# Weight splitting, staging copies and B/K scaling move between VectorE, ScalarE and GpSimd in a one-core hybrid decoder step, under another planner clock

## The chip, the cores and the metric

The program runs on 1 core of one Trainium2 chip. The metric is device microseconds of one execution; the times before are the median of three runs. The names of the engines in the profile are PE (TensorE matmul), PEld (TensorE weight load), DVE (VectorE), ACT (ScalarE), POOL (GpSimd) and SP (SyncE, which here only issues transfers).

## The reference

One step of a decoder layer for a 1024-token prompt and 8 sequences of 4 sampled tokens: one input projection feeds an RWKV-7 branch (a recurrence with a 64x64 state for each of 16 heads) and an RG-LRU branch; both are gated, merged, projected, normed and sent through a SwiGLU FFN.

```python
z = jnp.einsum('btd,de->bte', x, w_in)
...
# RWKV-7, for each token and head
sa = jnp.einsum('bhij,bhj->bhi', S, -kk_t)
S = (S * w_t[:, :, None, :]
     + sa[..., None] * (kk_t * a_t)[:, :, None, :]
     + v_t[..., None] * k_t[:, :, None, :])
y_t = jnp.einsum('bhij,bhj->bhi', S, r_t)
...
merged = (gate_a * yA + gate_b * yB).astype(x.dtype)
mix = jnp.einsum('bte,ed->btd', merged, w_o)
h1 = _layer_norm(ALPHA * x + mix, ln1_g, ln1_b)
ffn = (jax.nn.silu(h1 @ w_ffn_gate) * (h1 @ w_ffn_up)) @ w_ffn_down
y = _layer_norm(ALPHA * h1 + ffn, ln2_g, ln2_b)
```

Everything is fp32. The large products are made from two parts of each operand: a high part that TensorE's fast fp32 format holds, and the low part that is left; three products (high-high, high-low, low-high) are added up.

## The kernel before, in words

**Weights.** `Weights` streams weight tiles of 128x8x128 through two buffers `wraw`, loaded by transfers that the GpSimd queue issues. `split` cuts each tile in two halves of 128x512. ScalarE copies a half to the high part `wh` (`A`), then the low part `wl` is `wraw - wh`: by VectorE for half 0 (`TT`), by GpSimd for half 1 (`PTT`; `ON_POOL = 1,`). Weight tiles 0 to 115 belong to the input projection, 116 to 131 to the output projection `wo`, and the others to the FFN.

**The first part** (up to about 1475 us of the trace) makes the input projection in two passes, the first over samples and tokens 0 to 511 (matmuls of 300, 292 and 256 columns), the second over tokens 512 to 1023 (512 columns). `STREAM` lists the order of its groups as (kind, unit): kind 0 is `r` and `k`, 1 is `v`, 2 is the LRU's input, 3 the three gates; a unit is two 128-row channel blocks, that is four heads, in one pass, so that there are eight units. While TensorE works down this list, the recurrence of each unit runs beside it in steps:

- `wkv_tile` makes the decayed keys and queries on ScalarE and VectorE (tiles `tmp`, `rge`, `kta`).
- `stage(u, g)` copies them for half g of a unit (four chunks of 64 tokens) to `bk` and `arm`: for each of 2 blocks and 2 heads, ScalarE makes two copies of 64x256 and VectorE two (`TS` by 1.0). There are 16 such halves.
- `inverse(u, g)` makes products of these on TensorE, sends `nz` through DRAM (`scrN` to `bn`), solves 16x16 triangles on VectorE with 30 small operations (`btmp`, `bt`), and brings the result back through DRAM (`scrT` to `tdv`, `scrZ` to `zt`). These transfers go through SP's queue. In the lists below `scrN_172`, `scrT_176`, `scrZ_174` belong to half 0 and `scrN_173`, `scrT_177`, `scrZ_175` to half 1.
- `chain(u)` is the recurrence, 8 steps a unit. In a step TensorE makes `cx` from `arm` and the state `su`, ScalarE and VectorE copy it to `xs`, TensorE makes `cu`, both copy it to `su`, TensorE makes `cs_` from `bkt` and `su`, and VectorE adds four 64x64 pieces of the state for the next step. `ahead(c)` prepares step c: VectorE scales `bk` by a column of `pc` into `bkh` (twice 128x128), and TensorE transposes it.
- `finish`, `gate_out` and `lru` norm, gate and make the other branch. `bonus_weights` copies two tiles of 128x512 or 128x548 per unit to `rkk` on GpSimd.

`arm`, `bk` and `rb` have one buffer: a half is staged only once the chain of the unit before has passed the same half.

**The FFN** (1475 to 2190 us) is one dense run of matmuls with weight splitting beside it, and a last norm ends the program.

**Order.** No engine's order is written out. A planner (`Ticker`) emits the instructions of all tasks one by one; on each engine they run in the order in which they were emitted. It keeps a model of time (`Clock`): each instruction gets a cost, and the task whose next instruction could start earliest is emitted next. Between matmuls of the dense stream `tick` puts in what the model holds to be ready. Two parts of that model matter here: `clocked` doubles the cost of matmuls in a 3.413 us window after one with little work (a TensorE clock at half speed), and `shared` lengthens a VectorE operation by 0.7 of its overlap with one on GpSimd. Every instruction that the planner emits for a task has line L333 in the profile, those of the main stream L263; the buffers' names (`wl`, `bkh`) tell them apart.

Of the kernel before, what the change touches and what calls it, by code (L numbers as in the profile page):

```python
# [9 lines left out]
F32 = mybir.dt.float32  # L10
# [35 lines left out]
ON_POOL = 1,  # L46
G_RK, G_V, G_XB, G_GATE = range(4)
STREAM = [(0, 0), (1, 0), (1, 1), (0, 1), (2, 0), (3, 0), (0, 2), (2, 1), (3, 1), (0, 3), (2, 2), (1, 2), (3, 2), (2, 3), (1, 3), (3, 3), (0, 4), (1, 4), (1, 5), (0, 5), (2, 4), (3, 4), (2, 5), (0, 6), (3, 5), (2, 6), (2, 7), (0, 7), (1, 6), (3, 6), (1, 7), (3, 7)]
# [28 lines left out]
class Clock:  # L77
# [6 lines left out]
    def __init__(self):  # L84
        self.t = dict.fromkeys(("PE", "ACT", "DVE", "POOL", "SP", "DMA"), 0.0)
        self.uses = {}
        self.masks = {}
        self.table = 0
        self.tile = None
        self.port = {"DVE": [], "POOL": []}  # L90
        self.window, self.work, self.half = 0, 0.0, True
# [30 lines left out]
    def cost(self, e, f, out, ins, args, kw):  # L122
        n = max(self.size(x) for x in [out] + ins[:1])
        sbuf = all(x.space == SB for x in [out] + ins)
        if e == "PE":
            if f == "transpose":
                return 0.109
            k, m, n = args[1].shape[0], args[1].shape[1], self.size(args[2])
            if args[1].dtype == F32R:
                return max(0.11, n / 2250)  # L130
            if k <= 32:
                return 0.045
            return max(m, n) / 600 if m == 128 else max(0.09, n / 1000)
# [15 lines left out]
    WINDOW = 3.413  # L149

    def clocked(self, at, n, share):

        while at >= self.WINDOW * (self.window + 1):
            self.half = self.work < self.WINDOW * (0.7 if self.half else 0.45)
            self.window += 1
            self.work = 0.0
        n *= 1 + self.half
        self.work += min(n, self.WINDOW * (self.window + 1) - at) * share
        return n

    def shared(self, e, f, out, ins, at, end):

        if f == "memset" or e == "DVE" and (any(x.space != SB for x in ins) or f == "tensor_tensor_scan"):
            return 0.0
        port = self.port[e]
        port.append((at, end))
        del port[:-12]
        over = sum(max(0.0, min(end, b) - max(at, a)) for a, b in self.port["POOL" if e == "DVE" else "DVE"])
        if e == "DVE":
            return 0.7 * over  # L170
        self.t["DVE"] += 0.7 * over
        return 0.0
# [21 lines left out]
    def op(self, e, f, args, kw, at, last):  # L194
# [8 lines left out]
        else:  # L203
            if e == "PE":
# [4 lines left out]
                self.tile = tile  # L209
            end = at + self.FIXED[e] + self.cost(e, f, out, ins, args, kw)  # L210
            if e == "PE":
                share = 1.0 if min(tile) > 3 else 0.1 if max(tile) < 2 else 0.6
                end = at + self.clocked(at, end - at, share)
            if e in self.port:
                end += self.shared(e, f, out, ins, at, end)
# [147 lines left out]
def tile_hybrid_step(ctx: ExitStack, tc: tile.TileContext, I, O):  # L363
# [65 lines left out]
    class Weights:  # L429
# [21 lines left out]
        def split(self):  # L451
            for j, (_, nk) in enumerate(self.srcs):
# [3 lines left out]
                for part in range(self.PARTS):  # L456
                    k = slice(part * nk // self.PARTS, (part + 1) * nk // self.PARTS)
                    A(h[:, k], raw[:, k])
                    (PTT if part in ON_POOL else TT)(l[:, k], raw[:, k], h[:, k].bitcast(F32), OP.subtract)
# [35 lines left out]
    with ExitStack() as zctx:  # L495
# [240 lines left out]
        def bonus_weights(u, ts):  # L736
            while u > 0 and (u - 1, "fin") not in F:
                yield
            for i, t in enumerate(ts):
                pool.tensor_scalar(rkk[:, i, span(units[u][0])], t[:, span(units[u][0])], 1.0, None, op0=OP.mult)  # L740
                temps.put(t)
# [100 lines left out]
        def stage(u, g, n2, parts):  # L842
# [5 lines left out]
            for i, (t1, t4, t5) in enumerate(parts):  # L848
                cs, ts = slice(4 * g, 4 * g + 4), slice(PO + 256 * g, PO + 256 * g + 256)
                for h in range(2):  # L850
                    s = slice(64 * h, 64 * h + 64)
                    A(bk[s, i, cs, 1 - h, :], t1[s, ts].rearrange(ch, t=64))
                    TS(bk[s, i, cs, h, :], t4[s, ts].rearrange(ch, t=64), 1.0)
                    A(arm[s, i, cs, h, 0, :], kzs[u][s, i, ts].rearrange(ch, t=64))
                    TS(arm[s, i, cs, h, 1, :], rzs[u][s, i, ts].rearrange(ch, t=64), 1.0)
# [148 lines left out]
        def chain(u):  # L1004
# [7 lines left out]
            def ahead(c):  # L1012

                if c >= 0:
                    for i in range(2):
                        TS(bkh[:, i], bk[:, i, c], pc[:, i, c:c + 1], None, op0=OP.mult)
# [961 lines left out]
```

## Time and profile before

| | before |
|---|---|
| median of 3 runs | 2242.56 us (2242.42 to 2244.06) |
| the profiled execution | 2241.18 us, of which the profile's span 2239.2 us |
| instructions | 44150 |
| PE / PEld busy | 2094.6 us (94%) / 1805.1 us (81%) |
| DVE / ACT / POOL busy | 1303.2 us (58%) / 992.5 us (44%) / 592.5 us (26%) |
| mean granted TensorE clock | 0.950 |
| HBM | 132.45 MB read, 17.57 MB written, 67 GB/s |

The profile is of one execution. Shares of a whole span hide that the first part and the FFN differ; the views by stretch of time (windows) and the chain of waits tell them apart. In a row of a group, the number behind x is the count, then come the busy time in us and the mean of one in ns, then the idle time before it with what ended it. A fp32 matmul of the recurrence counts as two matmuls in the profile.

### The profile page before, as it was taken

The page shows a single profiled execution, that of the slowest core. Times are in us where ns is not written, and L with a number is a line of the kernel's source. Part 1 is how long each engine was busy: PE and PEld are TensorE (multiplying, and loading weights), DVE is VectorE, ACT ScalarE, POOL GpSimd, SP SyncE. Part 2 cuts the span into 40 slices and gives each one's busy share as a digit, 9 for nine tenths or more (in the row PEclk, how much of TensorE's full clock was granted, in tenths as well). Part 3 has the DMA queues.
Part 4 walks back from the last instruction along what each step waited for, and adds up shares of the span by engine and source line. Part 5 has one row for each costly group of instructions (what it writes and reads, how often), then busy time and mean ns, then how long its engine had stood idle before and what let it go on. Part 6 is the DMA issues. An engine that isn't in the chain of part 4 may idle for free.

```text
span 2239.2 us, 44150 instructions
## 1 busy us (share of the span) xinstructions
PE 2094.6 (94%) x17664; PEld 1805.1 (81%) x17664; DVE 1303.2 (58%) x3123; ACT 992.5 (44%) x2220; POOL 592.5 (26%) x961
## 2 busy tenths in 40 slices
PE   7899789989999999899989889999999999999997
PEld 6898688987977776666667678889999999999986
DVE  4785876986967476887967755632322322223227
ACT  4556555756555457556585433752112121121221
POOL 3331232331513331231422313221211211212124
PEclk9997899999979999989999989999999999999999
DMA  4131121231321232131322433211111111111111
GB/s 132 62 105 42 36 74 49 71 92 53 117 72 42 88 95 58 60 84 38 92 60 62 130 96 120 104 67 37 58 48 37 49 49 33 62 38 48 57 38 78
DMA packets 125564, 152.83 MB, mean 68 GB/s; under 512 B 82912, under 2 KB 87424, under 8 KB 125360
## 3 DMA queue, kind: packets, MB, share of 16 engines
q0 software_dynamic: 32576, 112.75, 14.9%
q1 hardware_dynamic: 92784, 37.28, 6.7%
q8 instruction: 138, 2.26, 0.4%
q14 instruction: 66, 0.54, 0.1%
HBM read 132.45 MB, written 17.57 MB: 67 GB/s over the span
## 4 chain that ended last, share of the span: by engine, by line
PE 65%; DVE 23%; ACT 7%; issue 3%; DMA 2%; POOL 0%; SPq 0%; POOLq 0%; DVEq 0%; ACTq 0%
PE bank L263 52%; PE bank L333 12%; DVE tmp L333 5%; DVE wl L333 2%; DVE arm L333 2%; DVE btmp L333 2%; DVE bt L333 2%; ACT tmp L333 1%; DVE yb L333 1%; DVE rge L333 1%; DVE su L333 1%; DVE bk L333 1%; ACT wh L333 1%; DVE rb L333 1%; ACT L333 1%
## 5 line engine op out<-in xcount | busy, mean ns | idle before, releaser
L263 PE MATMUL bank<-xx,wh 128*128 128x512 f32 (+4 forms) x3168 | 811.8, 343 | 32.7 <-ACT xx L263 8.6
L263 PEld LDWEIGHTS bank<-xx,wh 128*128 128x128 f32 x3168 | 553.4, 196 | 95.8 <-issue 19.0
L333 POOL TENSOR_TENSOR wl<-wraw,wh 128x512 fp32r<-128x512 f32 (+2 forms) x212 | 276.6, 1305 | 1178.0 <-ACT wh L333 1063.5
L263 PE MATMUL bank<-xx,wl 128*128 128x512 f32 (+4 forms) x1584 | 541.2, 342 | 0.3 <-DVE wl L333 0.3
L333 ACT ACTIVATE wh<-wraw 128x512 fp32r<-128x512 f32 (+2 forms) x424 | 249.9, 599 | 300.3 <-PE bank L263 265.7
L263 PE MATMUL bank<-hh,wh 128*128 128x272 f32 (+1 forms) x1056 | 341.8, 324 | 1.3 <-ACT hh L333 1.3
L263 PE MATMUL bank<-hl,wh 128*128 128x272 f32 (+1 forms) x1056 | 342.8, 325 | 0.2 <-DVE hl L333 0.2
L263 PE MATMUL bank<-hh,wl 128*128 128x272 f32 (+1 forms) x1056 | 341.9, 324 | 0.0
L263 PEld LDWEIGHTS bank<-xx,wl 128*128 128x128 f32 x1584 | 310.0, 196 | 31.2 <-issue 4.1
L333 DVE TENSOR_TENSOR wl<-wraw,wh 128x512 fp32r<-128x512 f32 (+1 forms) x212 | 187.5, 884 | 248.4 <-ACT wh L333 247.5
L263 PEld LDWEIGHTS bank<-hh,wh 128*128 128x128 f32 x1056 | 199.0, 188 | 18.1 <-ACT hh L333 1.8
L263 PEld LDWEIGHTS bank<-hl,wh 128*128 128x128 f32 x1056 | 198.9, 188 | 16.4 <-DVE hl L333 0.5
L263 PEld LDWEIGHTS bank<-hh,wl 128*128 128x128 f32 x1056 | 198.8, 188 | 15.5
L263 PE MATMUL bank<-u,wh 128*128 128x272 f32 (+1 forms) x864 | 197.5, 322 | 0.0
L263 PEld LDWEIGHTS bank<-u,wh 128*128 128x128 f32 x864 | 143.8, 188 | 12.9
L333 DVE TENSOR_TENSOR acc<-acc,bank 128x272 f32<-128x272 f32 (+3 forms) x120 | 62.2, 519 | 137.0 <-PE bank L263 135.2
L263 PE MATMUL bank<-u,wl 128*128 128x272 f32 (+1 forms) x432 | 139.4, 323 | 0.0
L333 DVE TENSOR_TENSOR sg<-sg,bank 128x272 f32<-128x272 f32 (+1 forms) x66 | 34.4, 521 | 159.7 <-PE bank L263 159.7
L333 ACT ACTIVATE sg<-bank 128x272 f32<-128x272 f32 (+1 forms) x66 | 30.7, 465 | 195.8 <-PE bank L263 195.8
L333 ACT ACTIVATE su<-bank 64x256 f32<-64x256 f32 (+1 forms) x192 | 60.0, 338 | 82.8 <-PE bank L333 78.8
L333 DVE SCALAR_TENSOR_TENSOR su<-su,pc,bank 64x64 f32<-64x64 f32 x224 | 62.7, 280 | 44.3 <-PE bank L333 39.3
L263 PEld LDWEIGHTS bank<-u,wl 128*128 128x128 f32 x432 | 81.2, 188 | 6.1
(249 smaller groups left out, 3185.4 us busy)
## 6 DMA issues: line engine op xcount, KB each, us to landing
wraw<-in_win POOLq DMA_DIRECT2D x116, 512.0 KB, 3.6
wraw<-in_wgu POOLq DMA_DIRECT2D x48, 512.0 KB, 3.6
wraw<-in_wo POOLq DMA_DIRECT2D x16, 512.0 KB, 3.6
wraw<-in_wdn POOLq DMA_DIRECT2D x24, 256.0 KB, 2.9
wraw<-in_wdn POOLq DMA_DIRECT2D x16, 320.0 KB, 3.2
mgd<-yb POOLq DMA_DIRECT2D x32, 128.0 KB, 2.5
out_y<-tmp SPq DMA_DIRECT2D x8, 512.0 KB
scrN<-nz SPq DMA_DIRECT2D x64, 32.0 KB
```

Source lines behind the costliest of these rows:

```text
L263: fn(*args, **kw)
L333: fn(*args, **kw)
```

## The change

Four pieces of work move and the planner's model changes:

- `split`: for weight tiles with j < `N_IN` = 132 (input projection and `wo`) both low halves are subtracted by VectorE; for the FFN's tiles half 1 stays on GpSimd.
- `stage`: the two VectorE copies become ScalarE copies, so that ScalarE makes all four.
- `ahead`: `bkh` is scaled by ScalarE (an activation with a scale column) instead of VectorE.
- `bonus_weights`: the copies to `rkk` go from GpSimd to ScalarE.
- `Clock`: the model of the half-speed TensorE clock goes (`clocked`); instead of a stretch by overlap, an operation of VectorE or GpSimd that uses the shared port waits until the one that holds it ends (`locked`). A cost of small matmuls changes from 0.09 to 0.08, and `STREAM` is another order of the same 32 groups.

```diff
-ON_POOL = 1,
+ON_POOL, N_IN = (1,), 132
 G_RK, G_V, G_XB, G_GATE = range(4)
-STREAM = [(0, 0), (1, 0), (1, 1), (0, 1), (2, 0), (3, 0), (0, 2), (2, 1), (3, 1), (0, 3), (2, 2), (1, 2), (3, 2), (2, 3), (1, 3), (3, 3), (0, 4), (1, 4), (1, 5), (0, 5), (2, 4), (3, 4), (2, 5), (0, 6), (3, 5), (2, 6), (2, 7), (0, 7), (1, 6), (3, 6), (1, 7), (3, 7)]
+STREAM = [(0, 0), (1, 0), (0, 1), (2, 0), (1, 1), (3, 0), (2, 1), (0, 2), (3, 1), (2, 2), (1, 2), (0, 3), (3, 2), (2, 3), (1, 3), (3, 3), (0, 4), (1, 4), (2, 4), (0, 5), (1, 5), (2, 5), (3, 4), (0, 6), (3, 5), (2, 6), (0, 7), (1, 6), (1, 7), (3, 6), (2, 7), (3, 7)]
...
-            return max(m, n) / 600 if m == 128 else max(0.09, n / 1000)
+            return max(m, n) / 600 if m == 128 else max(0.08, n / 1000)
...
-    WINDOW = 3.413
-
-    def clocked(self, at, n, share):
...
-    def shared(self, e, f, out, ins, at, end):
...
+    def locked(self, e, f, out, ins, at):
+
+        if f in ("memset", "tensor_reduce", "tensor_tensor_scan") or e == "DVE" and any(x.space != SB for x in [out] + ins):
+            return at, False
+        for a, b in self.port["POOL" if e == "DVE" else "DVE"]:
+            if a <= at < b:
+                at = b
+        return at, True
...
+            lock = False
+            if e in self.port:
+                at, lock = self.locked(e, f, out, ins, at)
             end = at + self.FIXED[e] + self.cost(e, f, out, ins, args, kw)
-            if e == "PE":
-                share = 1.0 if min(tile) > 3 else 0.1 if max(tile) < 2 else 0.6
-                end = at + self.clocked(at, end - at, share)
-            if e in self.port:
-                end += self.shared(e, f, out, ins, at, end)
+            if lock:
+                self.port[e] = self.port[e][-8:] + [(at, end)]
...
-                    (PTT if part in ON_POOL else TT)(l[:, k], raw[:, k], h[:, k].bitcast(F32), OP.subtract)
+                    (PTT if part in ON_POOL and j >= N_IN else TT)(l[:, k], raw[:, k], h[:, k].bitcast(F32), OP.subtract)
...
-                pool.tensor_scalar(rkk[:, i, span(units[u][0])], t[:, span(units[u][0])], 1.0, None, op0=OP.mult)
+                A(rkk[:, i, span(units[u][0])], t[:, span(units[u][0])])
...
-                    TS(bk[s, i, cs, h, :], t4[s, ts].rearrange(ch, t=64), 1.0)
+                    A(bk[s, i, cs, h, :], t4[s, ts].rearrange(ch, t=64))
...
-                    TS(arm[s, i, cs, h, 1, :], rzs[u][s, i, ts].rearrange(ch, t=64), 1.0)
+                    A(arm[s, i, cs, h, 1, :], rzs[u][s, i, ts].rearrange(ch, t=64))
...
-                        TS(bkh[:, i], bk[:, i, c], pc[:, i, c:c + 1], None, op0=OP.mult)
+                        A(bkh[:, i], bk[:, i, c], AF.Copy, pc[:, i, c:c + 1])
```

Because the planner sets the order, every engine's order changes. Three places follow. (In the changed file the planner's helper is line L316 instead of L333 and the main stream's L246 instead of L263.)

The first is SP's queue in unit 0. Before, half 1 (`scrN_173`) is sent out and its `bn` read back ahead of half 0 (`scrN_172`):

```order
L333 DMA scrN_173<-nz 32x8x32
L333 DMA tmp_96<-scrS 4x128
L333 DMA scrN_173<-nz 32x8x32 x3
L333 DMA scrX<-tmp_96 4x128
L333 DMA bn<-scrN_173 32x16x16 x2
L333 DMA zc_170<-scrX 32x2x4 x2
L333 DMA scrN_172<-nz 32x8x32
```

and in the changed kernel:

```order
L316 DMA scrN_172<-nz 32x8x32
L316 DMA tmp_94<-in_lora 128x256
L316 DMA scrN_172<-nz 32x8x32 x3
L316 DMA bn<-scrN_172 32x16x16 x2
L316 DMA scrS<-sc_169 32x2x4 x2
L316 DMA tmp_96<-scrS 4x128
L316 DMA scrN_173<-nz 32x8x32 x2
```

Half 0, on which the chain of unit 0 waits, now goes first.

The second is TensorE's queue at the first step of unit 3's chain, the last unit of the first pass. `su_149,arm` is `cx`, `xs,nz` is `cu`, `su_149,bkt_155` is `cs_`; rows with `xx` are the dense stream. Before:

```order
L333 MATMUL bank_71<-su_149,arm 64x64 x4
L333 MATMUL bank_68<-tdv,nz 32x16
L333 MATMUL bank_67<-tmp 128x256
L263 MATMUL bank_65<-xx,wh_78 128x292 x2
L333 MATMUL bank_70<-cst,vz_126 128x128 x2
L333 MATMUL bank_70<-cst,bkh 128x128 x2
L333 MATMUL bank_71<-xs,nz 64x64 x4
L333 MATMUL bank_68<-zt,p_139 32x16 x32
L333 MATMUL bank_68<-p_139,zt 32x16 x6
L333 MATMUL bank_71<-su_149,bkt_155 64x64 x4
```

and in the changed kernel, from a few rows behind `cx` on:

```order
L316 MATMUL bank_69<-tmp 128x256
L316 MATMUL bank_70<-cst,vz_126 128x128 x2
L316 MATMUL bank_70<-cst,bkh 128x128 x2
L316 MATMUL bank_71<-xs,nz 64x64 x4
L316 MATMUL bank_67<-tmp 32x64 x2
L246 MATMUL bank_66<-xx,wl_79 128x512
L246 MATMUL bank_66<-xx,wh_77 128x512
L316 MATMUL bank_68<-tmp 128x292
L246 MATMUL bank_66<-xx,wh_77 128x512
L246 MATMUL bank_66<-xx,wl_79 128x512
L246 MATMUL bank_66<-xx,wh_77 128x512 x2
L316 MATMUL bank_71<-su_149,bkt_155 64x64 x4
```

Before, the first pass's last tiles (292 columns) stand here; now the second pass's first tiles (512 columns) stand ahead of this chain and in it. Counted over all rows, the stream's matmuls between the last `cs_` of one chain and the first of the next, and within the chains, are:

| stretch of TensorE's order | before | after |
|---|---|---|
| ahead of chain 0 | 954 | 730 |
| chain 0 to chain 1 | 184 | 512 |
| chain 1 to chain 2 | 656 | 524 |
| chain 2 to chain 3 | 432 | 504 + 62 of 512 columns |
| chain 3 to chain 4 (512 columns, but 8 before) | 484 | 320 |
| in chains 0, 1, 2 | 150, 134, 150 | 188, 164, 162 |
| in chain 3 | 116 | 80 of 512 columns |
| in chains 4, 5, 6 (512 columns) | 100, 92, 108 | 130, 104, 120 |

The third is the same chain step on the engines that carry `bkh`. Before, VectorE's queue:

```order
L333 TENSOR_SCALAR bkh<-bk,pc_135 128x128 x2
L333 COPY xs<-bank_71 64x2x64
L333 TENSOR_SCALAR bkh<-bk,pc_135 128x128 x2
L333 COPY su_149<-bank_71 64x2x64
L333 SCALAR_TENSOR_TENSOR su_150<-su_149,pc_135,bank_71 64x64 x4
L333 TENSOR_TENSOR tdv<-tdv,bank_68 32x8x16 x2
```

In the changed kernel, ScalarE's queue:

```order
L316 ACTIVATE xs<-bank_71 64x2x64
L316 ACTIVATE bkh<-bk,pc_135 128x128
L316 ACTIVATE wh_78<-wraw_76 128x512
L316 ACTIVATE rge_199<-bank_65,omu 128x512
L316 ACTIVATE bkh<-bk,pc_135 128x128
L316 ACTIVATE tmp<-bank_67 32x64 x2
L316 ACTIVATE wh_78<-wraw_76 128x512
L316 ACTIVATE tmp_94<-bank_68,dv 128x292
L316 ACTIVATE tmp_94<-bank_69,dv 128x256
L316 ACTIVATE su_149<-bank_71 64x2x64
```

`bkh` now shares ScalarE's queue with the splitting of weights and with copies out of the stream's banks, and the second `bkh` stands behind one of each.

More of the change, by code (lines that the diff above doesn't have):

```diff
@@ L90, in __init__ @@
         self.port = {"DVE": [], "POOL": []}
-        self.window, self.work, self.half = 0, 0.0, True
     def mask(self, ap):
@@ L147, in cost @@
         return max(0.1, n / {"tensor_tensor": 450, "tensor_scalar": 330, "tensor_copy": 300}.get(f, 1150))
-    WINDOW = 3.413
-    def clocked(self, at, n, share):
[L153 to L159, printed above, removed]
-    def shared(self, e, f, out, ins, at, end):
[L163 to L172, printed above, removed]
+    def locked(self, e, f, out, ins, at):
[5 more added lines that the diff above has]
+        return at, True
     def accesses(self, args, kw):
```

## The prediction

> **What bounds the kernel now.** I read the page's engine shares and its chain of waits first, then the same by stretch of time, then the groups of VectorE, ScalarE and GpSimd in the first part, then single rows.
>
> ```profile
> PE 2094.6 (94%) x17664; PEld 1805.1 (81%) x17664; DVE 1303.2 (58%) x3123; ACT 992.5 (44%) x2220; POOL 592.5 (26%) x961
> PE 65%; DVE 23%; ACT 7%; issue 3%; DMA 2%; POOL 0%; SPq 0%; POOLq 0%; DVEq 0%; ACTq 0%
> 0.00:1475.00 1475.00, 1346.75 (x13047) 1129.15 (x13048) 1068.12 (x2723) 837.80 (x1907) 434.06 (x781) 0.93 0.26 78
> 1475.00:2190.00 715.00, 715.00 (x4360) 644.47 (x4359) 195.59 (x311) 146.99 (x297) 135.58 (x164) 1.00 0.15 47
> 1474.52 715.64 PE bank L263 x4359
> ```
>
> The second row is the chain of waits; the windows' columns are the stretch, its length, the busy time of PE, PEld, DVE, ACT and POOL, the granted clock, the DMA share and GB/s. From 1475 to 2190 us TensorE is busy all the time at full clock and is one piece of the chain. Nothing that the change touches bounds it there, and the FFN keeps its splitting. So VectorE's 23% of the chain (515 us) and ScalarE's 7% (157 us) lie nearly all in the first 1475 us: 35% and 11% of them. In that part VectorE is busy 72%, ScalarE 57%, and the clock is 0.93. The first part is bound by two things in turn: TensorE's own work, and the recurrence's way through VectorE, ScalarE and the transfers, which leaves TensorE with too little to do in places.
>
> **Work that moves, engine by engine.** Groups of the first part (to 1475 us), and one group of the whole span (48 halves of 128x256):
>
> ```profile
> L333 DVE TENSOR_TENSOR wl<-wraw,wh 128x512 fp32r<-128x512 f32 x138 | 110.2, 799 | 50.9 <-ACT wh L333 50.0
> L333 DVE TENSOR_SCALAR bkh<-bk,pc 128x128 f32<-128x128 f32 x128 | 37.4, 333 | 1.8
> L333 DVE TENSOR_SCALAR bk<-tmp 64x256 f32<-64x256 f32 x64 | 25.8, 407 | 0.9
> L333 DVE TENSOR_SCALAR arm<-rge 64x256 f32<-64x256 f32 x64 | 21.6, 341 | 0.6
> L333 ACT ACTIVATE wh<-wraw 128x512 fp32r<-128x512 f32 x276 | 171.4, 627 | 62.3 <-PE bank L263 48.4 <-issue 7.1 <-DMA wraw<-in_win 5.1
> L333 ACT ACTIVATE wh<-wraw 128x256 fp32r<-128x256 f32 x48 | 19.8, 416 | 109.2 <-PE bank L263 97.8 <-issue 11.4
> L333 ACT ACTIVATE bk<-tmp 64x256 f32<-64x256 f32 x64 | 25.8, 410 | 0.6
> L333 ACT ACTIVATE tmp<-tmp 128x512 f32<-128x512 f32 x35 | 21.9, 629 | 5.7 <-DVE tmp L333 5.2
> L333 ACT ACTIVATE tmp<-kta,vec 128x512 f32<-128x512 f32 x8 | 5.7, 717 | 0.0
> L333 POOL TENSOR_TENSOR wl<-wraw,wh 128x512 fp32r<-128x512 f32 x137 | 192.4, 1404 | 675.7 <-ACT wh L333 590.3 <-DVE bkh L333 22.4 <-DVE wl L333 13.8
> L333 POOL TENSOR_SCALAR rkk<-tmp 128x512 f32<-128x512 f32 x8 | 14.3, 1793 | 0.1
> L333 POOL TENSOR_SCALAR rkk<-tmp 128x548 f32<-128x548 f32 x8 | 13.1, 1644 | 0.2
> ```
>
> VectorE loses 37.4 + 25.8 + 21.6 = 84.8 us. It gains 132 subtractions. How long each will be shows in single rows:
>
> ```profile
> 7.75 0.69 DVE L333 TENSOR_TENSOR wl<-wraw,wh 128x512 fp32r<-128x512 f32 x1 [7.75 <-ACT wh L333]
> 19.01 1.16 DVE L333 TENSOR_TENSOR lora<-tmp,lora 64x256 fp32r<-64x256 f32 x1 [0.40 <-ACT lora L333]
> 230.49 0.29 DVE L333 TENSOR_SCALAR bk<-tmp 64x256 f32<-64x256 f32 x1
> 239.60 1.93 POOL L333 TENSOR_TENSOR wl<-wraw,wh 128x512 fp32r<-128x512 f32 x1 [12.19 <-ACT wh L333]
> 240.39 1.30 DVE L333 TENSOR_SCALAR bk<-tmp 64x256 f32<-64x256 f32 x1
> 1438.35 1.27 POOL L333 TENSOR_TENSOR wl<-wraw,wh 128x512 fp32r<-128x512 f32 x1 [2.64 <-ACT wh L333]
> 1438.40 1.77 DVE L333 TENSOR_TENSOR wl<-wraw,wh 128x512 fp32r<-128x512 f32 x1
> ```
>
> The same copy takes 0.29 us alone and 1.30 us while a GpSimd subtraction runs; a subtraction takes 0.69 us alone and 1.77 us beside one. Read row by row, 103 VectorE operations of the first part (one of the first is at 19.01, the last at 1438.40) lie over a GpSimd subtraction and are longer than their form alone, by 83 us together, and 21 more lie over `rkk` with 8.5 us. Some 17.5 us of these 91 sit in the 84.8 us that go anyway. So the 132 new subtractions cost 0.69 us each, 91 us, and 74 us of stretch vanish: VectorE's sum is -84.8 + 91 - 74 = -68 us of 1068. On the path I count it at VectorE's share of the chain, 35%: **-24 us**. If the path passes none of it, it is worth 0; if all, -68. The subtractions are hidden under the matmuls of the tile before; without that cover each would put 0.69 us on the path.
>
> ScalarE gains 128 copies of 64x256 by 0.410 (52 us); 128 `bkh`; and 16 `rkk` of 0.63 (10 us). No row shows `bkh` on ScalarE: its nearest is the one with a scale column, 717 ns at 512 columns, less 384 columns at (627 - 416) / 256 = 0.82 ns, so 0.40 us (between 0.33, VectorE's mean, and 0.72), 51 us. Together +113 us on 838. `bkh` and `rkk` at ScalarE's 11% of the chain: **+7 us**. The staging copies are no average load: a half had 8 copies on each engine side by side, and now has 16 in a row, 6.6 us instead of 3.3. Over 16 halves that is 52 us if each stands on the path and TensorE has nothing else; 0 if covered. I take a quarter, **+13 us**, since TensorE mostly has the stream, and the page's chain by line gives `bk` on VectorE but 1%:
>
> ```profile
> PE bank L263 52%; PE bank L333 12%; DVE tmp L333 5%; DVE wl L333 2%; DVE arm L333 2%; DVE btmp L333 2%; DVE bt L333 2%; ACT tmp L333 1%; DVE yb L333 1%; DVE rge L333 1%; DVE su L333 1%; DVE bk L333 1%; ACT wh L333 1%; DVE rb L333 1%; ACT L333 1%
> ```
>
> By the Trainium skill ("ScalarE: Activation LUTs", rules for kernel authors) multiplications belong on VectorE, not ScalarE; by this rule the 256 moved copies and scalings are a loss, which is the third rival below. The rows agree for one `bkh` (0.33 us against my 0.40); the busy shares, 72% and 57%, speak the other way for the whole.
>
> GpSimd loses 132 x 1.404 + 27.4 = 213 us. It holds 0% of the chain, so that counts at **0**. Transfers of weights are still issued by it, behind the last subtraction of the tile that frees the buffer, now on VectorE; `wh` waited only 5.1 us for such transfers, which covers a delay. Added waits of VectorE for `wh` (50 us idle for 138 before, so up to 48 for 132 more) hold up what is queued behind them, the state's updates among it; most of that stands in idle time (28%), and I leave it in the range.
>
> **Order.** Where TensorE had too little to do, the clock fell to half:
>
> ```profile
> 188.00:215.00 27.00, 26.46 (x377) 22.91 (x372) 16.88 (x47) 15.69 (x41) 3.31 (x4) 0.50 0.11 28
> 258.00:323.00 65.00, 51.04 (x669) 46.34 (x668) 54.61 (x172) 27.18 (x70) 18.64 (x49) 0.78 0.23 61
> 638.00:680.00 42.00, 40.89 (x588) 31.01 (x586) 19.84 (x66) 19.16 (x52) 2.17 (x4) 0.51 0.15 40
> 1287.00:1304.00 17.00, 13.67 (x178) 10.86 (x178) 7.25 (x23) 5.30 (x15) 0.00 (x0) 0.50 0.60 170
> 118.55 0.17 DVE L333 TENSOR_TENSOR btmp<-bn,bt 64x15 f32<-64x15 f32 x1 [0.22 <-POOL bt L333]
> 141.94 0.17 DVE L333 TENSOR_TENSOR btmp<-bn,bt 64x15 f32<-64x15 f32 x1
> 132.21 12.63 PE bank L263 x100
> 769.69 12.99 PE bank L263 x56
> 376.34 1.17 DVE L333 SCALAR_TENSOR_TENSOR sst<-su,pc,bank 64x64 f32<-64x64 f32 x4 [0.80 <-PE bank L333]
> 512.35 1.17 DVE L333 SCALAR_TENSOR_TENSOR su<-su,pc,bank 64x64 f32<-64x64 f32 x4 [2.43 <-PE bank L333]
> 713.03 1.16 DVE L333 SCALAR_TENSOR_TENSOR sst<-su,pc,bank 64x64 f32<-64x64 f32 x4 [0.83 <-PE bank L333]
> 873.99 1.21 DVE L333 SCALAR_TENSOR_TENSOR su<-su,pc,bank 64x64 f32<-64x64 f32 x4
> ```
>
> The four `btmp` and matmul rows are read with the order: the triangle of unit 0's half 1 begins at 118.55, half 0's at 141.94, and the two runs of matmuls give a matmul of the stream at full clock: 0.126 us in the first pass, 0.232 in the second. By the counts of the order:
>
> - From chain 0 to chain 1 (258 to 323 us) 184 become 512, that is 41 us more work. There TensorE lost 65 - 51 = 14 us idle and 0.22 x 65 = 14 us of clock: up to 28 us filled.
> - Ahead of and in chain 3 (638 to 680) matmuls of the second pass stand, 62 and 80 of them, 33 us, where the first pass ran out: 42 x 0.49 = 20 us to fill.
> - Ahead of chain 0, 224 fewer, 28 us less cover. But half 0 of unit 0 now goes first, so the chain can start 23 us earlier (141.94 - 118.55). A loss of 5 us.
> - Chain 1 to 2 has 132 fewer (17 us), chain 3 to 4 164 fewer (38 us): 55 us of cover gone, which costs all of it if these stretches then starve, nothing if they are long enough. I take half: these gaps were the longest, 136 us (376.34, the last update of chain 1's state, to 512.35, the first of chain 2) and 161 us (713.03 to 873.99).
> - 1287 to 1304 stays.
>
> That is -28 - 20 + 5 + 27 = **-16 us**, between -43 (none of the 55 felt) and +12 (all of it).
>
> By the Trainium skill ("TensorE: Matmul & The Clock Gate", part 1) TensorE's clock is throttled unless the last window was busy. The four windows agree. It speaks against this change, whose planner no longer knows it: matmuls in such a window take twice what is planned, and that is the second rival.
>
> **Sum** against the profiled execution (2241.2 us, 1.4 below the median): 2241.2 - 24 + 7 + 13 - 16 = 2221, as a median **2222 us**.
>
> **Rivals.**
>
> 1. *The starved windows go and the lighter VectorE shortens the path more.* For it: 35% of the first part's chain is VectorE. Against: TensorE was 91% busy there. -34 (half of 68) + 20 - 33 (the order with 10 us of the lost cover felt instead of 27) = -47, so 2196 us.
> 2. *The order slips (slower).* Chains 2 and 4 come when the stream between has run dry: all 55 us of lost cover are felt, TensorE falls to half clock there, and the order is worth +12 us instead of -16; and the new fill at 258 to 323 outlasts the wait by 41 - 28 = 13 us, which holds chain 1 up. -4 + 12 = +8, and with half of the 13 us some +14: 2257 us. It decides from about 40 us of lost cover felt. For it: the clock model that went; against: the length of those gaps.
> 3. *ScalarE is the bound (slower).* The staging copies stand in a row on the path in all 16 halves: -24 + 7 + 52 - 16 = +19, so 2262 us. It decides from about 33 us, 2 us a half. For it: `bkh` and the chain's copies stand behind weight copies, which had 48.4 us of waiting for TensorE. Against: ScalarE goes to some 64% of the first part, VectorE stays above.
> 4. *It does nothing*: what an engine gains stands in idle time and the path is TensorE's. 2242 us.
>
> **How the numbers follow.** Forecast 0.46 (2206 to 2236), rival 1 0.16, rival 2 0.13, rival 3 0.13, rival 4 0.12. About 0.2% (4.5 us) is what a measurement can tell from no change. Faster 0.62, same 0.12, slower 0.26. The range 2190 to 2258 leaves out rival 3 and little of rival 1.
>
> **What would show it.** Right: VectorE's `wl` at 0.69 us and no stretched copies in the first part; VectorE near 1000 us there, ScalarE near 950; full clock at the places of 258 to 323 and 638 to 680; first triangle of half 0 about 20 us earlier. Wrong: half-clock windows ahead of chains 2 and 4; staging that takes over 10 us a half with `bk` on ScalarE in the chain of waits; waits of TensorE for `bkh` above those of before (total, times, longest):
>
> ```profile
> PE bank L333 <- DVE bkh L333: 9.8, 13, 2.7
> ```

## The result, and the profile after

The changed kernel takes **2156.55 us** (median of four, 2147.47 to 2162.81) against 2242.77 us for the kernel before on the same chip: a ratio of 0.961 (95% interval 0.957 to 0.965), 86 us less. The prediction was 2222 us, from 2190 to 2258. The direction was right; the gain is four times the forecast and lies below the range. The profiled execution took 2161.04 us (span 2159.3), 4.5 us above its median.

The page's engine shares and its chain of waits, by engine and by line, after the change:

```profile
PE 2057.3 (95%) x17664; PEld 1782.9 (83%) x17664; DVE 1239.0 (57%) x2999; ACT 1072.5 (50%) x2491; POOL 395.7 (18%) x813
PE 74%; DVE 11%; ACT 9%; issue 3%; DMA 1%; POOL 1%; POOLq 0%; SPq 0%; DVEq 0%; ACTq 0%
PE bank L246 60%; PE bank L316 15%; DVE tmp L316 2%; ACT tmp L316 2%; DVE wl L316 1%; ACT wh L316 1%; DVE su L316 1%; ACT L316 1%; ACT nz L316 1%; DVE btmp L316 1%; ACT arm L316 1%; DVE bt L316 1%; ACT bk L316 1%; DVE arm L316 1%; DVE rge L316 1%
```

VectorE's share of the chain fell from 23% to 11%, and TensorE took over. The long last piece of TensorE (the FFN) begins at 1392.85 us instead of 1474.52 and is as long as before (714.1 against 715.6):

```profile
1392.85 714.12 PE bank L246 x4359
```

So all of the gain, 82 us, lies in the first part. Where in TensorE's row? I cut both kernels at the last matmul of the output projection, the same 12775 matmuls but for one (windows; columns as before). First the kernel before, then after:

```profile
0.00:1437.00 1437.00, 1310.64 (x12774) 1094.90 (x12775) 1045.88 (x2673) 802.73 (x1830) 426.61 (x773) 0.93 0.26 77
```

```profile
0.00:1356.00 1356.00, 1275.34 (x12775) 1074.21 (x12776) 978.96 (x2549) 882.80 (x2101) 229.91 (x625) 0.95 0.27 82
```

TensorE's busy time fell by 35 us for the same matmuls (the clock, 0.93 to 0.95), and its idle time from 126 to 81 us (1437 - 1310.64, 1356 - 1275.34), 46 us. The change moved nothing on TensorE itself, so both come from when the others let it work, and from what stands in its queue when they don't. Summed over the trace's records of the granted clock in these two stretches, half speed lasted 212 us before and 137 us after. Below, the "half-clock time" of a run is this sum.

Groups of the first part after, to 1393 us, by form:

```profile
L316 DVE TENSOR_TENSOR wl<-wraw,wh 128x512 fp32r<-128x512 f32 x269 | 184.9, 690 | 67.6 <-ACT wh L316 63.1 <-PE bank L246 2.5
L316 ACT ACTIVATE wh<-wraw 128x512 fp32r<-128x512 f32 x275 | 171.6, 626 | 50.6 <-PE bank L246 33.5 <-issue 5.9 <-DMA wraw<-in_win 5.5
L316 ACT ACTIVATE bk<-tmp 64x256 f32<-64x256 f32 x128 | 47.1, 407 | 1.0
L316 ACT ACTIVATE bkh<-bk,pc 128x128 f32<-128x128 f32 x128 | 44.7, 391 | 0.2
L316 ACT ACTIVATE rkk<-tmp 128x548 f32<-128x548 f32 x8 | 5.1, 659 | 0.1
```

The subtraction's mean fell from 799 to 690 ns: the stretch is gone.

### The profile page after: what moved, and what is told of

It is laid out like the page before. It is cut to its first block, busy times and chain, and to the rows that moved or that the text cites. A ratio compares the mean times of both kernels' runs of the same rounds, so it can differ in the third digit from the quotient of the medians.

```text
span 2159.3 us, 44129 instructions
## 1 busy us (share of the span) xinstructions
PE 2057.3 (95%) x17664; PEld 1782.9 (83%) x17664; DVE 1239.0 (57%) x2999; ACT 1072.5 (50%) x2491; POOL 395.7 (18%) x813
## 4 chain that ended last, share of the span: by engine, by line
PE 74%; DVE 11%; ACT 9%; issue 3%; DMA 1%; POOL 1%; POOLq 0%; SPq 0%; DVEq 0%; ACTq 0%
PE bank L246 60%; PE bank L316 15%; DVE tmp L316 2%; ACT tmp L316 2%; DVE wl L316 1%; ACT wh L316 1%; DVE su L316 1%; ACT L316 1%; ACT nz L316 1%; DVE btmp L316 1%; ACT arm L316 1%; DVE bt L316 1%; ACT bk L316 1%; DVE arm L316 1%; DVE rge L316 1%
## 5 line engine op out<-in xcount | busy, mean ns | idle before, releaser
L246 PE MATMUL bank<-xx,wh 128*128 128x512 f32 (+4 forms) x3168 | 801.0, 340 | 28.6 <-ACT xx L246 9.1
L246 PEld LDWEIGHTS bank<-xx,wh 128*128 128x128 f32 x3168 | 547.3, 194 | 89.8 <-ACT xx L246 9.0
L246 PE MATMUL bank<-xx,wl 128*128 128x512 f32 (+4 forms) x1584 | 537.1, 339 | 0.0
L316 DVE TENSOR_TENSOR wl<-wraw,wh 128x512 fp32r<-128x512 f32 (+1 forms) x344 | 263.2, 767 | 265.3 <-ACT wh L316 260.8
L316 ACT ACTIVATE wh<-wraw 128x512 fp32r<-128x512 f32 (+2 forms) x424 | 250.7, 599 | 287.1 <-PE bank L246 248.0
L246 PE MATMUL bank<-hl,wh 128*128 128x272 f32 (+1 forms) x1056 | 342.4, 324 | 0.9 <-DVE hl L316 0.9
L246 PE MATMUL bank<-hh,wh 128*128 128x272 f32 (+1 forms) x1056 | 341.0, 323 | 0.5 <-ACT hh L316 0.5
L246 PE MATMUL bank<-hh,wl 128*128 128x272 f32 (+1 forms) x1056 | 341.3, 323 | 0.0
L246 PEld LDWEIGHTS bank<-xx,wl 128*128 128x128 f32 x1584 | 307.2, 194 | 28.2 <-issue 3.0
L246 PEld LDWEIGHTS bank<-hh,wh 128*128 128x128 f32 x1056 | 198.6, 188 | 17.3 <-ACT hh L316 1.2
L246 PEld LDWEIGHTS bank<-hl,wh 128*128 128x128 f32 x1056 | 198.6, 188 | 17.2 <-DVE hl L316 1.5
L246 PEld LDWEIGHTS bank<-hh,wl 128*128 128x128 f32 x1056 | 198.5, 188 | 15.4
L316 POOL DMA_DIRECT2D wraw<-in_win x114 | 61.9, 543 | 778.4 <-DVE wl L316 480.7
L246 PE MATMUL bank<-u,wh 128*128 128x272 f32 (+1 forms) x864 | 197.5, 322 | 0.0
L316 POOL TENSOR_TENSOR wl<-wraw,wh 128x512 fp32r<-128x512 f32 (+2 forms) x80 | 90.5, 1131 | 525.6 <-ACT wh L316 502.8
L246 PEld LDWEIGHTS bank<-u,wh 128*128 128x128 f32 x864 | 143.9, 188 | 12.9
L316 DVE TENSOR_TENSOR acc<-acc,bank 128x272 f32<-128x272 f32 (+3 forms) x120 | 62.2, 519 | 140.7 <-PE bank L246 138.9
L246 PE MATMUL bank<-u,wl 128*128 128x272 f32 (+1 forms) x432 | 139.4, 323 | 0.0
L316 ACT ACTIVATE sg<-bank 128x272 f32<-128x272 f32 (+1 forms) x66 | 30.8, 466 | 195.8 <-PE bank L246 195.8
L316 DVE TENSOR_TENSOR sg<-sg,bank 128x272 f32<-128x272 f32 (+1 forms) x66 | 34.4, 521 | 157.5 <-PE bank L246 157.4
L316 ACT ACTIVATE u<-sg 128x272 fp32r<-128x272 f32 (+1 forms) x66 | 33.1, 502 | 114.2 <-DVE sg L316 114.2
L316 ACT ACTIVATE su<-bank 64x256 f32<-64x256 f32 (+1 forms) x192 | 60.2, 337 | 59.3 <-PE bank L316 57.0
```

The source lines that it names most:

```text
L246: fn(*args, **kw)
L316: fn(*args, **kw)
```

## The experiments

The theory to test was the one of the prediction, that the moved work pays and the new order adds a little. The rival: the order that the planner now emits brings most of it, and the moved work little.

### Order and engines apart

A wrapper lets an instruction be planned for one engine and run on another, so that every queue keeps its order while the work moves. e1 keeps the order of before and runs the moved work where the change puts it:

```diff
-  PTT(l[:, k], raw[:, k], h[:, k].bitcast(F32), OP.subtract)
+  tk.do("POOL", (nc.vector if j < 132 else nc.gpsimd).tensor_tensor, "tensor_tensor", ...)
-  TS(bk..., 1.0); TS(arm..., 1.0); TS(bkh..., op0=OP.mult); pool.tensor_scalar(rkk...)
+  # planned as before, executed as nc.scalar.activation
```

> The order of the kernel before on TensorE and SP, instruction by instruction, but the moved work runs on its new engines: all low halves of the first part on VectorE, staging copies, bkh and rkk on ScalarE (the planner still books them on the old engines). Theory E (engines): the lighter VectorE and the freed shared port carry most of the 86 us, so about 2175 us (2160 to 2195). Theory O (order): the new order carries it, so 2225 to 2245 us. Theory B (both are needed, each is half): about 2200 us.

e2 is the counterpart: the order of the changed kernel, the work on the engines of before.

> The mirror image: the changed kernel's order on TensorE and SP, but half 1 of the low parts and rkk run on GpSimd, staging copies of two kinds and bkh on VectorE as before. Theory E: stretched VectorE operations are back, so 2220 to 2245 us. Theory O: the order keeps the gain, 2160 to 2180 us. Theory B: about 2200 us.

e1 took 2260.7 us (ratio 1.0064, 1.0044 to 1.0085), e2 2180.8 (0.9719, 0.9694 to 0.9744). **The order alone gains 62 us of the 86. The engines gain 24 us in the new order, and lose 18 in the old one** (medians; by the interval of e1 it is 10 to 19). The windows to the end of the output projection, e1 and then e2:

```profile
0.00:1455.00 1455.00, 1317.55 (x12788) 1100.61 (x12789) 982.30 (x2551) 891.51 (x2105) 207.88 (x626) 0.92 0.26 77
```

```profile
0.00:1381.00 1381.00, 1284.54 (x12779) 1078.59 (x12780) 1039.51 (x2674) 802.01 (x1830) 437.58 (x773) 0.95 0.28 81
```

In e1 VectorE is 64 us lighter than before (982 against 1046), as promised, and TensorE's idle time still rises, from 126 to 137 us. Part of why is in the waits of TensorE for `bkh` (total, times, longest): before 9.8 us, here

```profile
PE bank L333 <- ACT bkh L406: 16.5, 13, 2.4
```

In that order `bkh` stands on ScalarE behind work that was placed there without it. In the changed kernel's own order weight copies stand ahead of it too, but TensorE hardly waits:

```profile
PE bank L316 <- ACT bkh L316: 2.3, 4, 1.1
```

### Which of the moves pay, with the order held

e11 is the changed kernel's order with only GpSimd's share back (half 1 of the low parts, `rkk`); e12 has only the staging copies and `bkh` back on VectorE.

```diff
 # e11
+  tk.do("DVE", (nc.gpsimd if part in ON_POOL else nc.vector).tensor_tensor, "tensor_tensor", ...)   # j < N_IN
+  on_pool(rkk...)    # planned as ACT
 # e12
+  on_dve(bk...); on_dve(arm...); on_dve(bkh..., pc...)   # planned as ACT
```

> The changed kernel with its order on every queue held; only the low parts of half 1 of the first part's weight tiles and the copies to rkk are executed on GpSimd, as before; bkh and the staging copies stay on ScalarE. With all four pieces back this order takes 2181 us, with none 2157. Theory P (the 24 us come from the stretch that GpSimd's work causes on VectorE): 2175 to 2190 us, with VectorE's operations stretched by some 70 us again. Theory L (they come from the 85 us of copies and scalings taken off VectorE): 2155 to 2165 us.

> The changed kernel with its order on every queue held; only the two staging copies a block and head and bkh are executed on VectorE, as before; the subtractions and rkk stay as in the changed kernel. Theory P (stretch): 2150 to 2162 us, since nothing overlaps a GpSimd subtraction in the first part. Theory L (load of VectorE): 2172 to 2185 us. My sum took the staging copies in a row on ScalarE for a loss of 13 us and bkh with rkk for 7: by that it would fall to some 2140 to 2150 us.

e11 took 2159.4 us (0.9638, 0.9612 to 0.9663), e12 2155.4 (0.9609, 0.9593 to 0.9626); the changed kernel is at 0.9611, e2 at 0.9719. Both theories fell, since each had expected a loss in one of the two runs. Read from e2, where all the work is on the engines of before, either half of the moves brings nearly the whole gain: the copies and `bkh` alone 21 us (e11), GpSimd's share alone 25 (e12). The other half then adds nothing measurable (3 and -1 us, and the intervals leave some 10 us either way).

e11 has the stretch back, some 80 us of it read row by row against the same forms alone, and hardly pays for it. One row of e11, the first step of a triangle beside a GpSimd subtraction, then the same form alone in the changed kernel:

```profile
433.24 0.78 DVE L316 TENSOR_TENSOR btmp<-bn,bt 64x15 f32<-64x15 f32 x1
```

```profile
105.21 0.16 DVE L316 TENSOR_TENSOR btmp<-bn,bt 64x15 f32<-64x15 f32 x1
```

In the window of e11 to the end of the output projection, VectorE is busy 970 us, nearly as long as in the changed kernel (979), with 132 subtractions fewer:

```profile
0.00:1349.00 1349.00, 1263.82 (x12776) 1062.26 (x12777) 970.38 (x2417) 874.28 (x2085) 432.95 (x773) 0.96 0.29 83
```

VectorE has slack enough for the stretch or for the copies, not for both on the operations that TensorE waits for. That is my reading: of the 24 us, waits for `bkh` (9.6 us in e2, 7.2 in e12, 1.9 in e11, 2.3 in the changed kernel) show a part, and the rest is not traced.

### Which part of the planner makes the order

Now the moves are kept, and parts of the planner are put back into the changed kernel, which then emits its own order. e3: all of the old model (half-speed windows, stretch, 0.09). e4: the old `STREAM`. e5: half-speed windows and 0.09. e6: the stretch instead of the lock. e8: only 0.09.

```diff
+  end = at + self.clocked(at, end - at, share)      # e3, e5
+  end += self.shared(e, f, out, ins, at, end)       # e3, e6, in place of locked
-  STREAM = [(0, 0), (1, 0), (0, 1), (2, 0), ...]    # e4
+  STREAM = [(0, 0), (1, 0), (1, 1), (0, 1), ...]    # e4
-  max(0.08, n / 1000)                               # e3, e5, e8
+  max(0.09, n / 1000)                               # e3, e5, e8
```

> The changed kernel (new engines, new STREAM) planned with the whole old clock: half-speed TensorE windows and stretch by overlap. Theory E: the clock hardly matters, 2155 to 2180 us. Theory O, where the order comes from the clock: 2210 to 2240 us. Theory O, where it comes from STREAM: 2155 to 2180 us; the next run tells these apart.

> The changed kernel with the new clock and engines, but the old STREAM. Theory E: 2155 to 2180 us. Theory O through STREAM (more of the stream between chains 0 and 1, the second pass begun ahead of chain 3): 2200 to 2235 us. Theory O through the clock: 2155 to 2180 us.

> The changed kernel, only with the planner's half-speed TensorE windows put back (and the 0.09 that went with them); the port lock stays. Theory H (the half-speed model spoiled the order): as with the whole old clock, 2215 to 2235 us, and fewer of the stream's matmuls within the chains. Theory L (the lock model made the order better): 2155 to 2175 us.

> The changed kernel, only with the stretch by overlap back in the planner instead of the lock; no half-speed windows. Theory H: 2150 to 2175 us, since GpSimd has hardly anything left in the first part that could overlap. Theory L: 2210 to 2230 us.

> The changed kernel with the one small constant put back (0.09 instead of 0.08 for small matmuls). It tells how far any small change of the plan moves the time: if orders are robust, 2150 to 2170 us; if the plan is a lottery in which the changed kernel drew well, 2175 to 2210 us, and then differences of 20 us between plans carry no reason of their own.

| run | what is put back | us | ratio, 95% interval |
|---|---|---|---|
| e3 | half speed, stretch, 0.09 | 2227.0 | 0.9922 (0.9900 to 0.9944) |
| e5 | half speed, 0.09 | 2223.9 | 0.9905 (0.9886 to 0.9925) |
| e8 | 0.09 | 2172.0 | 0.9680 (0.9666 to 0.9694) |
| e6 | stretch for lock | 2172.3 | 0.9686 (0.9670 to 0.9703) |
| e4 | old `STREAM` | 2191.8 | 0.9766 (0.9741 to 0.9790) |

The lock, which the change names, is worth 16 us by this one pair. e5 and e8 differ in the half-speed model alone: 52 us. But e8 against the changed kernel (15 us for 0.09 instead of 0.08, a number without a meaning at this size) warned that plans scatter, so that one pair proves little. e13 and e18 put the half-speed model back with costs of 0.08 and 0.085, e14 is the changed kernel with 0.085:

> The changed kernel with the half-speed model put back and nothing else (the cost of small matmuls stays 0.08). 160 us of stream in the chains. If the 52 us found between two kernels that differ only in this model are its doing, the time is 2195 to 2240 us here too. If any two plans differ by so much by chance (theory C), it may come out anywhere between 2150 and 2225 us.

> The changed kernel with a cost of small matmuls of 0.085 instead of 0.08: a change of the plan without a meaning, to see how far plans of the same model scatter (0.08 gave 2157 us, 0.09 gave 2172). 182 us of stream in the chains. If the model decides: 2150 to 2180 us. Theory C: as far out as 2200 us.

> The changed kernel with the half-speed model back and a small cost of 0.085; the third plan of this model and this STREAM (0.08 gave 2240 us, 0.09 gave 2224), beside 2157, 2172 and 2176 without the model. 157 us of stream in the chains. If the model does it: 2215 to 2245 us, with half-clock time above 200 us. By chance (theory C): below 2195 us.

| | plans (us) | mean | half-clock time (us) |
|---|---|---|---|
| planner with half speed | e3 2227, e5 2224, e13 2240, e18 2189 | 2220 | 232, 212, 266, 188 |
| planner without | changed 2157, e6 2172, e8 2172, e14 2176 | 2169 | 137, 154, 137, 147 |

e18 missed its expectation of 2215 to 2245 by 26 us and came in where theory C, chance, had put it, and the plans of one kind lie up to 51 us apart. But the slowest plan without the model is 13 us faster than the fastest with it, and the means differ by 51. The changed kernel is the fastest plan of all that were run and may have been picked for that; without it the mean of the others is 2174, and 46 us remain. With `STREAM` and engines as in the changed kernel, then, the half-speed model did harm, by some 50 us in the mean of four plans each, and any one plan carries a chance of some 20 to 30 either way. What it does to TensorE, in e13 to the end of the output projection:

```profile
0.00:1435.00 1435.00, 1325.58 (x12778) 1104.55 (x12779) 978.50 (x2549) 887.70 (x2102) 229.14 (x625) 0.91 0.27 78
```

Against the changed kernel's row TensorE is busy 50 us longer for the same matmuls and idle 29 us more (109 against 81), while VectorE and ScalarE do the same work within 5 us. The granted clock falls from 0.95 to 0.91. **The planner that reckons with half speed makes more of it.** Set beside the times that this planner itself had reckoned when it emitted the order of e13, 181 matmuls of the stream were planned at half speed and 173 ran so, but only 84 were the same ones: the model had the amount about right and the place wrong half of the time.

### Without the moves

e7 is the kernel before with only the new clock and 0.08; e17 has the new `STREAM` too, so that it is all of the change but the moves.

```diff
-  end = at + self.clocked(...); end += self.shared(...)   # the kernel before
+  at, lock = self.locked(e, f, out, ins, at)              # e7, e17
-  max(0.09, n / 1000)                                     # the kernel before
+  max(0.08, n / 1000)                                     # e7, e17
+  STREAM = [(0, 0), (1, 0), (0, 1), (2, 0), ...]          # e17
```

> The kernel before (old engines, old STREAM) with only the planner's clock changed. If the clock's gain does not need the other parts: new clock with the old STREAM gave 2192, and the old engines in the new order cost 24, so 2205 to 2225 us. If the clock helps only with the new engines: 2235 to 2255 us.

> The kernel before with the new clock, cost and STREAM, its work left on the engines of before, and planned so: all of the change but the moves between engines. 162 us of stream in the chains. Held in the order of the changed kernel, the old engines take 2181 us; planned for themselves, with the old STREAM, 2224. If the planner's model is what counts: 2175 to 2200 us. If the moves are needed for a good plan (VectorE's operations then wait in the plan for those of GpSimd): 2205 to 2230 us.

e7 took 2223.7 us (0.9912, 0.9893 to 0.9932), e17 2187.9 (0.9769, 0.9745 to 0.9792). All of the change but the moves thus gains 53 us. `STREAM` is worth 36 us here (e7 to e17) and 35 with the moves (e4 to the changed kernel), twice the same though each is one pair. With the old `STREAM` and the old engines the new clock alone gave only 20, where beside the new `STREAM` and engines the half-speed model alone cost some 50. That the two parts of the planner need each other is my reading of these single plans; it is not shown.

### How the model does it: two theories, neither of which held

The changed kernel runs more of the stream beside the recurrence: the matmuls of the stream inside the eight chains come to 184 us at full clock, in the kernel before to 157. So I thought that a planner which overrates TensorE's time puts too little of the stream there. e9 and e10 multiply all of TensorE's planned times by 1.2 and 0.9, e16 by 0.95, without half-speed windows:

```diff
+  if e == "PE":
+      end = at + 1.2 * (end - at)      # e10: 0.9, e16: 0.95
```

> The changed kernel, with one edit: the planner takes every instruction of TensorE to last 1.2 times as long as its cost says; no half-speed windows. The emitted order then has 165 us of stream matmuls within the eight chains, against 184 in the changed kernel and 157 in the kernel before. Theory S (a planner that overrates TensorE's time puts too little of the stream beside the chains, and the stretches that it feared come from that): it loses like the run with the half-speed model back, 2195 to 2225 us, with half-clock time above 180 us. Theory I (only the irregular doubling in windows, which stand at the wrong places, did harm; an even overrating is harmless): 2155 to 2180 us.

> The changed kernel, with one edit: the planner takes every instruction of TensorE to last 0.9 times as long as its cost says. The emitted order has 204 us of stream matmuls within the chains. Theory S: the stream beside the chains still pays, 2130 to 2157 us, with half-clock time below 137 us. Theory I, or a stream that by now holds up the chains: 2160 to 2190 us.

> The changed kernel with TensorE's planned times multiplied by 0.95; 190 us of stream in the chains. If the times lie on a curve through 0.9 (2189), 1.0 (2157) and 1.2 (2263): 2160 to 2180 us. Theory C (plans scatter by chance): anything from 2145 to 2200 us.

| factor | 0.9 (e10) | 0.95 (e16) | 1 (changed) | 1.2 (e9) |
|---|---|---|---|---|
| us | 2188.6 | 2177.2 | 2156.6 | 2263.5 |
| ratio, 95% interval | 0.9755 (0.9741 to 0.9770) | 0.9713 (0.9698 to 0.9728) | 0.9611 (0.9571 to 0.9651) | 1.0089 (1.0073 to 1.0105) |
| stream in chains, us | 204 | 190 | 184 | 165 |

With a factor of 1.1 (e15) the kernel took 2203.6 us, but one of its outputs was wrong (relative error 0.05), so it is left out of the table; the cause was not looked for.

Overrating hurts, beyond what I expected: an even 1.2 costs 107 us, more than the half-speed model, so the misplaced windows are not needed for the harm, and the theory that an even overrating is harmless fell. Underrating brought nothing either, with more of the stream in the chains: it costs 21 and 32 us, the first of which a number without a meaning can cost too. And e17 has only 162 us there with 133 us of half clock. The amount of stream beside the chains therefore isn't the cause. That the order is best where the planner's TensorE keeps about the chip's pace fits these runs, but is not shown, since the changed kernel is the fastest plan of all and any change of it is likely to look like a loss. Where in a plan the harm arises, matmul by matmul, stays open.

## Why the prediction was wrong

**The failed step is the order: -16 us, measured -62 (e2).** Inside it, the lost cover (+27) had the wrong sign, and the stretches from chain 4 on, which gained most, had no term but "1287 to 1304 stays". To see it I add up, by stretch, what TensorE loses: its idle time, and half of the time that it is busy at half clock. This is an estimate from the traces of the three kernels, over the first part up to the end of the output projection; what is left of TensorE's time is 1215 to 1218 us in all three. The sum falls by 57 us in e2, whose median is 62 us lower. A gap runs from the last update of one chain's state to the first of the next.

| stretch | order, predicted | lost before | in e2 (the order alone) | in the changed kernel |
|---|---|---|---|---|
| ahead of chain 0 | +5 | 42.0 | 39.2 | 37.7 |
| gap from chain 0 to 1 | -28 | 23.5 | 10.1 | 6.9 |
| gap from chain 2 to 3, and chain 3 | -20 | 25.4 | 21.1 | 10.4 |
| gaps from chain 1 to 2 and 3 to 4 | +27 | 33.0 | 21.7 | 18.4 |
| in chains 0, 1, 2 | none | 18.7 | 18.3 | 24.5 |
| from chain 4 on | none | 77.5 | 53.1 | 43.0 |
| sum | -16 | 220 | 163 | 141 |

- *The 55 us of cover taken out of chain 1 to 2 and chain 3 to 4 (+27).* The loss there fell by 11 us in e2. The gaps themselves shrank, from 136 to 99 us (394.38 to 493.77) and from 161 to 111 (719.16 to 829.67). The updates that bound them in the changed kernel, then the windows of the kernel before, then those of the changed one:

```profile
394.38 1.16 DVE L316 SCALAR_TENSOR_TENSOR sst<-su,pc,bank 64x64 f32<-64x64 f32 x4
493.77 1.16 DVE L316 SCALAR_TENSOR_TENSOR su<-su,pc,bank 64x64 f32<-64x64 f32 x4
719.16 1.17 DVE L316 SCALAR_TENSOR_TENSOR sst<-su,pc,bank 64x64 f32<-64x64 f32 x4 [0.57 <-PE bank L316]
829.67 1.22 DVE L316 SCALAR_TENSOR_TENSOR su<-su,pc,bank 64x64 f32<-64x64 f32 x4 [1.26 <-PE bank L316]
```

```profile
376.00:512.00 136.00, 126.35 (x1377) 117.05 (x1375) 111.65 (x298) 91.09 (x207) 46.26 (x91) 0.97 0.27 80
713.00:874.00 161.00, 147.92 (x1068) 115.42 (x1065) 110.81 (x240) 88.67 (x172) 55.47 (x76) 0.96 0.27 82
```

```profile
394.00:492.00 98.00, 91.92 (x1053) 87.27 (x1050) 80.96 (x242) 64.70 (x159) 19.52 (x57) 0.97 0.32 89
719.00:829.00 110.00, 104.81 (x792) 80.06 (x790) 89.62 (x203) 77.64 (x163) 19.13 (x47) 0.95 0.31 90
```

  In both kernels TensorE is busy 92 to 95% of these gaps at 0.95 to 0.97 of the clock: it did not starve there, with the cover or without it. That does not make TensorE what set their length. The chain of waits of the kernel before, from 376 to 512 us, has these lines of the program first (the view is limited in width); added up by engine it is 57% VectorE and 21% TensorE:

```profile
by line: DVE tmp L333 14.0%; PE bank L263 11.3%; PE bank L333 10.1%; issue 7.4%; DVE wl L333 6.2%; DVE bt L333 4.9%; DVE btmp L333 4.5%; DVE arm L333 4.4%; DVE rge L333 4.2%; DMA out_wkv_s<-tmp 3.1%; DMA tmp<-scrS 2.9%; DVE kta L333 2.9%; D
```

  From 713 to 874 us it is 39% VectorE and 51% TensorE; in the two gaps of the changed kernel TensorE has 52% and 64%. VectorE, too, had less to do in them afterwards (81 and 90 us instead of 112 and 111). Whether TensorE's work or the way through VectorE made these gaps long is not shown. Nor is a shorter gap a gain by itself, since what is taken out of it stands elsewhere: the gap from chain 0 to 1 grew from 64 to 99 us (229.6 to 328.6), with TensorE busy in it:

```profile
229.00:328.00 99.00, 94.43 (x1092) 88.46 (x1094) 77.54 (x231) 64.25 (x159) 22.25 (x68) 0.98 0.33 92
```

- *Ahead of chain 0 (+5 net).* The first triangle of half 0 began at 105.21 us instead of 141.94, 37 us earlier where I counted 23, and the first update of a state at 158.22 instead of 204.01:

```profile
158.22 1.22 DVE L316 SCALAR_TENSOR_TENSOR su<-su,pc,bank 64x64 f32<-64x64 f32 x4
```

  Hardly any of these 46 us is a gain. The loss ahead of the chain fell by 3 us in e2; the rest is the work of the matmuls that now stand later.

- *The starved places (-28 and -20).* Right as places, too large in size: the loss fell by 13 and 4 us in e2, by 17 and 15 with the moves. 258 to 323 runs at full clock with 3.4 us idle instead of 14, 638 to 680 at 0.92 instead of 0.51. Other places stay at half speed or become so:

```profile
258.00:323.00 65.00, 61.58 (x820) 57.60 (x821) 55.40 (x177) 39.09 (x92) 10.89 (x32) 1.00 0.39 101
638.00:680.00 42.00, 37.77 (x559) 28.77 (x558) 33.72 (x104) 26.28 (x71) 3.76 (x7) 0.92 0.22 65
324.00:338.00 14.00, 14.00 (x149) 12.30 (x149) 7.65 (x17) 9.26 (x22) 0.53 (x1) 0.51 0.00 1
1208.00:1229.00 21.00, 20.11 (x340) 16.69 (x340) 12.09 (x28) 13.85 (x34) 0.54 (x1) 0.51 0.50 143
```

  I had read half clock as TensorE with too little to do. By the rows it need not be idle for that: from 324 to 338 it is busy all the time at 0.51, and in the prediction's rows 26.46 of 27 us at 0.50 and 40.89 of 42 at 0.51.

- *From chain 4 on (no term).* The loss fell by 24 us in e2 and by 35 with the moves, the largest part. I had read one row there. What in the order did it is not traced.

That the order came out as a gain at all in my sum was in part luck: two fills that were rated too high outweighed a loss of cover that was not there.

**The engines: -24 + 7 + 13 = -4 predicted, -24 measured in the new order, +18 in the old.** The busy times were right: 690 ns a subtraction (0.69 predicted), 391 ns a `bkh` (0.40), 0.64 us an `rkk` (0.63), VectorE 1003 us of the first part (1000), ScalarE 919 (950):

```profile
0.00:1395.00 1395.00, 1312.90 (x13054) 1109.65 (x13055) 1002.89 (x2599) 919.36 (x2181) 238.12 (x634) 0.95 0.27 82
```

What failed is their conversion to time by a share of the chain. A share has no one price: the same moves were worth -24 and +18 in two orders, and each half of them 21 to 25 us with the other undone and nothing measurable with it done. The staging in a row (+13) cost nothing measurable, by e12. From the first start to the last, a half's copies to `bk` took 4.4 to 10.7 us, before 2.9 to 11.1, which suggests that their inputs set their pace and not ScalarE.

**The rivals.** *Order slips* rested on the premise that a planner that no longer knows the half-speed clock falls into it. It is reversed (e13). The Trainium skill ("TensorE: Matmul & The Clock Gate", part 1) has the array at half speed by default and at full speed after a busy window of about 3.4 us. The records of the granted clock before and after agree in the step, since half speed lasts 3.41 us or a multiple of it in the first part; but the row of 324 to 338 us has half speed for 14 us with TensorE busy throughout, so that busy time by the profile is not what decides, and "the four windows agree" in the prediction said too much. What the clock counts as busy, no run here shows. In any case a planner that models the half speed gave worse orders here than one that doesn't. *ScalarE the bound*: not shown by any run; only in the old order (e1) do the moves to it lose, and there by 18 us in all. *One big gain* (2196) had its direction, windows filled and a shorter path, but with the engines as its larger part. *Nothing* is out.

## What to carry to other kernels

Before the work in a stretch between two links of a serial chain is called cover, add up what TensorE loses there, by idle time and by half clock, and read the chain of waits: where TensorE is 93% busy, work moved out shortens the stretch and lengthens another, and only the loss can be gained. Do it for every stretch, not for the few that look worst. When a planner emits the order, hold the order and move the work, and hold the engines and change the order: here the edits that the change's list begins with were a quarter of the gain, and the time model and the list of groups together most of the rest. When two moves are tested, test each alone from both ends: here either alone brought what both brought. Compare a planner's models over several plans each, varied by a number without a meaning; one plan of each can differ by 15 to 50 us here for nothing.

## What the runs showed of the hardware

- GpSimd's work stretched VectorE's by some 80 us in the first part of e11, and that cost the kernel 3 us, within the noise. The same work on GpSimd cost 25 us where VectorE had its copies as well (e2 against e12): a long operation on an engine that has slack is not yet a loss.
- The same matmuls take TensorE longer in another order, by the clock alone: for the same 12775 matmuls, give or take four, its busy time was 1275 us at a mean clock of 0.95 and 1326 us at 0.91 (e13).
- A busy TensorE can stay at half clock: from 324 to 338 us of the changed kernel it was busy all 14 us, with 149 matmuls, many of them of 64x64 and 32x32, at 0.51.
